# Two blocks of conditioned mixers and expert layers on one core: convolution taps without GpSimd, residual rows scaled in other stages

## The chip, the cores and the metric

The kernel runs on one core of a Trainium2 chip. The metric is the device time of one execution in microseconds. Engines are named TensorE (PE in the rows), VectorE (DVE), ScalarE (ACT), GpSimd (POOL) and SyncE (SP, which only issues DMAs and takes part in no arithmetic).

## The reference

512 tokens of width 1024 pass a first block (a state space and attention mixer, then an expert layer) and a second block of two layers, each with a mixer and an expert layer. The second block has 256 context tokens beside the 512. What the change touches:

```python
def conv_mixers(h, w_in, w_out, a_dw_w, a_dw_b, a_ln_g, a_ln_b, b_dw_w):
    z = h @ w_in
    a_val, a_gate, b_gate, c_gate, b_val = jnp.split(z, CONV_SPLITS, axis=-1)
    ya = a_val * jax.nn.sigmoid(a_gate)
    ya = depthwise_conv(ya, a_dw_w) + a_dw_b          # 31 taps, 512 channels
    ya = jax.nn.silu(layer_norm(ya, a_ln_g, a_ln_b))
    yb = b_gate * depthwise_conv(c_gate * b_val, b_dw_w)   # 3 taps
    return jnp.concatenate([ya, yb], axis=-1) @ w_out
...
# second block, each layer
x_lat = layer_norm(DEEPNORM_ALPHA_2 * x_lat + g1 * y_lat, ln1_g[i], ln1_b[i])
h_lat = x_lat * (1.0 + sc2) + sh2
...
y = hier_moe(h_lat.reshape(-1, d), *moe_w).reshape(x_lat.shape)
x_lat = layer_norm(DEEPNORM_ALPHA_2 * x_lat + g2 * y, ln2_g[i], ln2_b[i])
```

The expert layer picks one group of experts and two experts in it for each token, so each expert of width 512 sees its own few tokens. The first layer norm's result is wanted twice: modulated, by the experts, and as it is, as the residual of the second norm. The residual rows are this result with gain and bias (`ln`) multiplied and added.

## The kernel before

Weights stay f32 in memory; for the projections a weight tile and its input are split into a rounded high part (`wh`, `xh`, ScalarE) and the rest (`wl`, `xl`, VectorE, the subtraction of L245), and three matmuls (`xh` `wh`, `xl` `wh`, `xh` `wl`) replace one. All weights are loaded in pieces of 128 x 2048 f32 (1 MB) by SyncE, in program order, into `raw` (four buffers) and, in the expert layers, `rawx` (eight more).

The span in order: mixer 1 (0 to 350), expert layer m1 (selection 366 to 388, run to 694, combination 698 to 748), `conv_layer` (748 to 1003) and its output projection, m2 (selection 1090 to 1138, run to 1697, combination to 1780), grouped query attention (`G.attend`), the projection for neighbourhood attention (`na_proj`) and that attention (`na`, 2066 to 2157), output projection, m3 (selection 2226 to 2265, run to 2690), final combination.

*Convolution.* `proj(u)` computes unit u of the input projection for four blocks of 128 channels, over 512 latent and 256 context columns (L1445, L1446). Unit 0 is a gate, unit 1 makes `AB`, the padded input of the 31 taps. The first `POOL_TAPS` = 7 taps are done by GpSimd, a product and a sum each (L1500, L1502), into a second accumulator; VectorE does the other 24 (L1505, L1508) and adds the two (L1511). Units 2 to 4 go on beside the taps; a scheduler has set the order of each engine, and VectorE's accumulates alternate with the `wl` subtractions of later units.

*Expert layers.* `Moe.start` opens pools and starts the first loads, `select` computes the routing and the index tables `midx`, `mtok`, `midn`, and `run` goes over S places, S = 32 in m2 and 26 in m3. An expert with few tokens has a place of H rows ("narrow", H = 32 in m2 and m3), the others 128 rows ("wide"); two or three places are double. The weights of the first two places, experts 0 and 1, are loaded before the routing is known, and they are wide in any case. A wide place cuts its weights into `wh` and `wl`, a narrow one multiplies gate and up weights straight from the loaded slot (L1208). GpSimd gathers a place's token rows (L1110, three buffers `xg`) and scatters its results (L1187 wide, L1238 narrow). `run` calls `step` so that gather, loads and matmuls of neighbouring places overlap, and calls `beside` once, at j = 10.

*Residual rows.* In `affine_rows` the function `keep` scales a tile of 128 normed rows on GpSimd with gain and bias (L1406, L1407); for m2 and m3 it is called between `start` and `select`, and for m2 the result goes to `xd2` in DRAM (L1409), where the end of the run picks it up. The residual of the convolution layer is scaled in m1's combination (L1900, L1901) and stored to `x2d`. The residual of the attention layer lies in `x3d`, and is loaded and scaled in `na` (L2021 to L2023).

## Time and profile before

| | us |
|---|---|
| median of 3 runs | 2746.97 (2745.14 to 2748.28) |
| the profiled execution, its own time | 2732.68 |
| its span | 2731.0 |
| TensorE busy | 2296.8 (84%) |
| VectorE busy | 1630.4 (60%) |
| ScalarE busy | 1075.3 (39%) |
| GpSimd busy | 541.5 (20%) |
| DMA, mean over the span | 244 GB/s, 666 MB |
| mean granted clock of TensorE | 0.921 |

Busy time counts from an instruction's start to its end, also where it stands still in between. A stage's limit is therefore read in the stage: which engine is busy all along, or which wait ends last there. In the rows "[6.36 <-DVE pt L663]" says that the engine sat idle for 6.36 us before this instruction and that VectorE's write of `pt` at line 663 ended it. Counts like "x6" group instructions that follow each other without a gap.

### The profile page before, as it was taken

To read this page: it belongs to the slowest core of one execution; us is meant where nothing else is said; L and a number is where in the kernel's file an instruction comes from. 1 tells how busy PE (TensorE), PEld (TensorE's weight loads), DVE (VectorE), ACT (ScalarE), POOL (GpSimd) and SP (SyncE) were. 2 spreads that over 40 slices of the span, in tenths; PEclk is the share of its full clock that TensorE was granted. 3 is DMA by queue.
4 is the path that set the end of the run, shared out by engine and by line. 5 is a ranking of instruction groups with operands and counts; after the bars stand their busy time and mean duration, and the time that the engine had idled before them with its cause. 6 is when DMAs were issued, how large, how long until landed. Compare 5 with 4: busy or idle time off the path is not lost. (4 is left out here: it accounts for less than half of the span.)

```text
span 2731.0 us, 33393 instructions
## 1 busy us (share of the span) xinstructions
PE 2296.8 (84%) x12255; PEld 1565.0 (57%) x12255; DVE 1630.4 (60%) x2357; ACT 1075.3 (39%) x1564; POOL 541.5 (20%) x479
## 2 busy tenths in 40 slices
PE   8999979998597799399988988399997757989991
PEld 6845547555286657276655655255684456766661
DVE  5536467454649967785455445666557687444445
ACT  4432237454411143175455445433322325444442
POOL 0122011100339513411111110110003131111112
PEclk9999989999798899699999999699998878999996
DMA  5222579998421145599999897621234346999993
GB/s 191 96 86 70 199 285 380 389 363 306 173 80 59 35 166 195 223 360 420 363 409 400 325 394 274 231 95 62 97 120 145 129 185 260 391 417 412 421 416 140
DMA packets 115257, 666.43 MB, mean 244 GB/s; under 512 B 21229, under 2 KB 22489, under 8 KB 44944
## 3 DMA queue, kind: packets, MB, share of 16 engines
q1 hardware_dynamic: 86960, 604.02, 56.9%
q10 hardware_dynamic: 11712, 30.81, 3.4%
q0 software_dynamic: 16416, 29.41, 3.0%
q8 instruction: 99, 1.62, 0.2%
q14 instruction: 70, 0.57, 0.1%
HBM read 646.27 MB, written 45.38 MB: 253 GB/s over the span
## 5 line engine op out<-in xcount | busy, mean ns | idle before, releaser
L245 DVE TENSOR_TENSOR wl<-raw,wh 128x1024 fp32r<-128x1024 f32 (+1 forms) x241 | 298.1, 1272 | 269.1 <-ACT wh L244 266.7
L245 DVE TENSOR_TENSOR wl<-rawx,wh 128x1024 fp32r<-128x1024 f32 x312 | 367.3, 1222 | 148.3 <-ACT wh L244 145.6
L272 PE MATMUL ps<-wh,xh 128*128 128x512 f32 (+1 forms) x864 | 335.4, 417 | 66.4 <-ACT wh L244 60.1
L273 PE MATMUL ps<-wl,xh 128*128 128x512 f32 (+1 forms) x864 | 352.0, 407 | 15.3 <-DVE wl L245 14.5
L244 ACT CAST wh<-rawx 128x1024 fp32r<-128x1024 f32 x312 | 311.3, 1049 | 94.6 <-PE ps L274 35.6
L274 PE MATMUL ps<-wh,xl 128*128 128x512 f32 (+1 forms) x864 | 346.2, 402 | 1.1 <-DVE xl L245 1.1
L244 ACT CAST wh<-raw 128x1024 fp32r<-128x1024 f32 (+1 forms) x241 | 244.4, 1051 | 187.5 <-PE ps L274 61.3
L272 PEld LDWEIGHTS ps<-wh,xh 128*128 128x128 f32 x864 | 168.7, 200 | 131.5 <-ACT wh L244 82.6
L273 PEld LDWEIGHTS ps<-wl,xh 128*128 128x128 f32 x864 | 172.1, 199 | 62.7 <-DVE wl L245 29.4
L274 PEld LDWEIGHTS ps<-wh,xl 128*128 128x128 f32 x864 | 171.3, 199 | 35.9 <-DVE xl L245 2.2
L1286 PE MATMUL adaps<-raw,ccs 128*2 128x512 f32 x352 | 165.0, 595 | 1.3 <-ACT adrow L1289 1.3
L1110 POOL DMA_INDIRECT xg<-xr,mtok x79 | 83.3, 1055 | 372.7 <-PE ps L1197 196.1
L273 PE MATMUL ps<-wl,ah 128*128 128x512 f32 x352 | 143.0, 406 | 13.8 <-DVE wl L245 13.8
L272 PE MATMUL ps<-wh,ah 128*128 128x512 f32 x352 | 142.1, 404 | 11.1 <-ACT wh L244 9.3
L274 PE MATMUL ps<-wh,al 128*128 128x512 f32 x352 | 137.7, 394 | 0.2 <-DVEq L1085 0.2
L1508 DVE SCALAR_TENSOR_TENSOR acc<-AB,cols,acc 128x783 f32<-128x783 f32 x92 | 130.7, 1463 | 0.5
L245 DVE TENSOR_TENSOR xl<-ps,xh 128x512 fp32r<-128x512 f32 x88 | 58.2, 687 | 107.6 <-ACT xh L244 107.5
L1185 ACT COPY y<-ps 128x512 f32<-128x512 f32 x88 | 51.7, 588 | 129.8 <-PE ps L274 129.8
L272 PE MATMUL ps<-wh,MH 128*128 128x512 f32 x224 | 90.0, 406 | 13.0 <-ACT wh L244 13.0
L273 PE MATMUL ps<-wl,MH 128*128 128x512 f32 x224 | 90.6, 404 | 3.3 <-DVE wl L245 3.2
L274 PE MATMUL ps<-wh,ML 128*128 128x512 f32 x224 | 90.5, 404 | 0.0
L272 PEld LDWEIGHTS ps<-wh,ah 128*128 128x128 f32 x352 | 66.7, 190 | 40.5 <-ACT wh L244 19.8
(583 smaller groups left out, 4387.1 us busy)
## 6 DMA issues: line engine op xcount, KB each, us to landing
rawx<-in_m_dram SPq DMA_DIRECT2D x296, 1024.0 KB
raw<-in_m_dram SPq DMA_DIRECT2D x148, 1024.0 KB
raw<-in_ada_dram SPq DMA_DIRECT2D x44, 1024.0 KB
raw<-in_w_dram SPq DMA_DIRECT2D x10, 1024.0 KB
raw<-in_cw_dram SPq DMA_DIRECT2D x10, 1024.0 KB
raw<-in_aw_dram SPq DMA_DIRECT2D x8, 1024.0 KB
xr<-rh SPq DMA_DIRECT2D x14, 512.0 KB
yt<-m2y SPq DMA_DIRECT2D x6, 1024.0 KB
```

The costliest lines, as they stand in the source:

```text
L244: self.nc.scalar.copy(hi, src)
L245: self.nc.vector.tensor_sub(lo, src, hi.bitcast(F32))
L272: nc.tensor.matmul(ps, ah, bh, start=start, stop=False)
L273: nc.tensor.matmul(ps, ah, bl, start=False, stop=False)
L274: nc.tensor.matmul(ps, al, bh, start=False, stop=stop)
L1110: nc.gpsimd.indirect_dma_start(out=xg[-1], out_offset=None, in_=self.xrows, in_offset=bass.IndirectOffsetOnAxis(ap=gi[0:n], axis=0), bound ...
L1185: nc.scalar.copy(y[:, h * 512:(h + 1) * 512], p)
L1286: nc.tensor.matmul(p[0:2], K.cc[:, k], raws[k // 4][:, (k % 4) * 512:(k % 4 + 1) * 512], start=k == 0, stop=k == 7)
L1508: nc.vector.scalar_tensor_tensor(acc[:, cb], AB[:, cb, j:j + 783], K.col("adw", j * 4 + cb), acc[:, cb], op0=OP.mult, op1=OP.add)
```

## The change

It has five parts.

1. Convolution: the first `PE_TAPS` = 4 taps are matmuls with a diagonal matrix of the tap's weights on TensorE (`taps`), which ScalarE builds and whose sums it writes to `acc` with the bias; VectorE does the other 27. GpSimd does none. The pool of the cut weight quarters has six buffers instead of four.
2. The residual rows of the convolution layer leave m1's combination unscaled and are loaded, scaled and stored again after unit 0 of the convolution's projection (`between`).
3. The residual rows of m2 go to `xd2` unscaled, behind each tile's norm; from j = 10 of m2's run on, each j loads one tile, scales it on GpSimd and stores it (`leave`, `keep`). m3's tiles are scaled at the same j, where they lie. The buffers `cuts` of m2 become five.
4. x3's rows are loaded, scaled and stored at the end of `G.attend`; `na` only loads them, on SyncE's queue.
5. `few=True` in m2 and m3: the first two places are narrow (an overflow goes to further blocks). In `select` two loops over tiles become single instructions.

```diff
-POOL_TAPS = 7
+PE_TAPS = 4
...
     def run(self, res, pre, beside=lambda j: None):
...
-            if j == 10:
-                beside()
+            beside(j)
...
-        nar = i is not None and self.P <= i < self.S
+        nar = i is not None and (self.P <= i < self.S or self.few and i < 2)
...
-    def keep():
-        nc.gpsimd.tensor_mul(r, r, K.gb[0])
-        nc.gpsimd.tensor_add(r, r, K.gb[1])
+    def keep(pool=None):
+        v, x = r, xd if xd is None else xd[t * 128:(t + 1) * 128]
         if xd is not None:
-            K.stores.append(lambda: nc.sync.dma_start(xd[t * 128:(t + 1) * 128], r))
+            v = pool.tile([128, D], F32, name="kept")
+            nc.sync.dma_start(v, x)
+        nc.gpsimd.tensor_mul(v, v, K.gb[0])
+        nc.gpsimd.tensor_add(v, v, K.gb[1])
+        if xd is not None:
+            nc.sync.dma_start(x, v)
     K.rows.push(lambda: rows(nc.vector))
+    if xd is not None:
+        nc.sync.dma_start(xd[t * 128:(t + 1) * 128], r)
...
-        S_ = Scope(tc, "c0s", bufs=4)
+        S_ = Scope(tc, "c0s", bufs=6)
...
+            def taps(cb):
+
+                dg = W.tile([128, PE_TAPS, 128], F32, name="diag", bufs=2)
+                p, q = K.ps(), K.ps()
+                for j in range(PE_TAPS):
+                    nc.scalar.mul(dg[:, j], K.ident, K.col("adw", j * 4 + cb))
+                    for d, o, n in ((p, j, T), (q, j + 527, TC)):
+                        nc.tensor.matmul(d[:, 0:n], dg[:, j], AB[:, cb, o:o + n], start=j == 0, stop=j == PE_TAPS - 1)
+                nc.scalar.activation(acc[:, cb, 0:T], p, AF.Identity, bias=K.col("adb", cb))
+                nc.scalar.activation(acc[:, cb, 527:783], q[:, 0:TC], AF.Identity, bias=K.col("adb", cb))
...
             proj(0, gate(AF.Sigmoid))
+            between(W)
             proj(1, aval)
+            taps(3)
...
-            for j in range(POOL_TAPS + 1, 31):
+            for j in range(PE_TAPS, 31):
...
-        for cb in range(4):
-            nc.vector.tensor_add(acc[:, cb], acc[:, cb], a2[:, cb])
...
-    m2 = Moe(K, 6, 32, 8, A["m2"], A["rw2"], A["rb2"], xr2, "m2", 32, 18, 32, 2)
-    m3 = Moe(K, 4, 32, 8, A["m3"], A["rw3"], A["rb3"], xr3, "m3", 26, 11, 32, 3, cuts=4)
+    m2 = Moe(K, 6, 32, 8, A["m2"], A["rw2"], A["rb2"], xr2, "m2", 32, 18, 32, 2, cuts=5, few=True)
+    m3 = Moe(K, 4, 32, 8, A["m3"], A["rw3"], A["rb3"], xr3, "m3", 26, 11, 32, 3, cuts=4, few=True)
...
+        def between(W):
+            gb = [K.bcast(W, A["ln"][i:i + 1], D, "gb%d" % i) for i in (2, 3)]
+            for t in range(4):
+                r = W.tile([128, D], F32, name="x2")
+                x = tile_of(x2d)(t)
+                nc.sync.dma_start(r, x)
+                nc.gpsimd.tensor_mul(r, r, gb[0])
+                nc.gpsimd.tensor_add(r, r, gb[1])
+                nc.sync.dma_start(x, r)
...
+    def leave(j, li, pool=None):
+        if j == 10:
+            K.gb = raw_rows([A["ln"][i:i + 1] for i in (li, li + 1)])
+        if j >= 10 and K.left:
+            K.left.pop(0)(pool)
...
                 G.attend(W, Oc)
+                gb3 = ln_rows(W, 6)
+                for t in range(4):
+                    r, x = W.tile([128, D], F32, name="x3", bufs=2), x3d[t * 128:(t + 1) * 128]
+                    nc.sync.dma_start(r, x)
+                    nc.gpsimd.tensor_mul(r, r, gb3[0])
+                    nc.gpsimd.tensor_add(r, r, gb3[1])
+                    nc.sync.dma_start(x, r)
...
-            nc.scalar.dma_start(x3r[64 * i:64 * i + 64, t], x3d.rearrange("(c r) d -> r c d", r=8)[2 * t + i])
-        nc.gpsimd.tensor_mul(x3r[:, t], x3r[:, t], got["gb3"][0])
-        nc.gpsimd.tensor_add(x3r[:, t], x3r[:, t], got["gb3"][1])
+            nc.sync.dma_start(x3r[64 * i:64 * i + 64, t], x3d.rearrange("(c r) d -> r c d", r=8)[2 * t + i])
```

The order on GpSimd ahead of m2's run, before: `lnrs` are steps of the norm, `xt` the rows of the convolution layer's result, `rh` gain and bias, `xg0` to `xg2` the buffers of the gather.

```order
L291 TENSOR_TENSOR lnrs_7564<-lnrs_7564,mhalf_101 128x1
L1406 TENSOR_TENSOR xt_6978<-xt_6978,rh_7677 128x1024 x4
L1407 TENSOR_TENSOR xt_6978<-xt_6978,rh_7679 128x1024 x4
L1406 TENSOR_TENSOR xt_6978<-xt_6978,rh_7677 128x1024 x2
L1407 TENSOR_TENSOR xt_6978<-xt_6978,rh_7679 128x1024 x2
L1110 DMA xg0_7698<-xr2_115,mtok_98 128x1024
```

The same place on GpSimd after the change.

```order
L1041 MEMSET xg1_7703 128x1024
L1041 MEMSET xg2_7704 128x1024
L288 TENSOR_SCALAR lnrs_7571<-lnmv_7569 128x1
L289 TENSOR_TENSOR lnrs_7571<-lnrs_7571,mhalf_99 128x1
L1109 DMA xg0_7702<-xr2_113,mtok_96 32x1024
```

The twelve scaling operations have left the place between the norm and the first gather, and this gather fetches 32 rows.

On GpSimd in m2's run, about the first double place, before: `m2y` is what the layer's results are scattered to, through `midx` by wide places and `midn` by narrow ones.

```order
L1238 DMA m2y_121<-y_9515,midn_100 6144x256
L1110 DMA xg0_7698<-xr2_115,mtok_98 128x1024
L1187 DMA m2y_121<-y_9647,midx_97 1536x1024
L1110 DMA xg1_7699<-xr2_115,mtok_98 32x1024
L1187 DMA m2y_121<-y_9657,midx_97 1536x1024
L1238 DMA m2y_121<-y_9865,midn_100 6144x256
```

After the change, the same place; `kept` is a reloaded tile, `rawx_9434` the slot with gain and bias.

```order
L1237 DMA m2y_119<-y_9323,midn_98 6144x256
L1109 DMA xg0_7702<-xr2_113,mtok_96 128x1024
L1409 TENSOR_TENSOR kept_9437<-kept_9437,rawx_9434 128x1024
L1410 TENSOR_TENSOR kept_9437<-kept_9437,rawx_9434 128x1024
L1186 DMA m2y_119<-y_9463,midx_95 1536x1024
L1109 DMA xg1_7703<-xr2_113,mtok_96 32x1024
L1186 DMA m2y_119<-y_9473,midx_95 1536x1024
L1409 TENSOR_TENSOR kept_9610<-kept_9610,rawx_9434 128x1024
L1410 TENSOR_TENSOR kept_9610<-kept_9610,rawx_9434 128x1024
```

Pairs of scaling operations stand between gathers and scatters, six in all; the second one stands behind the second scatter of the double place.

On SyncE at the same stage of m2's run, after the change; before, only the weight loads (`in_m2_dram`) stand there.

```order
L1876 DMA rawx_9434<-in_ln_dram 128x1024 x2
L1408 DMA kept_9437<-xd2_117 128x1024
L232 ISA
L232 DMA rawx_9482<-in_m2_dram 128x2048
L232 ISA
L232 DMA raw_9484<-in_m2_dram 128x2048
L1412 DMA xd2_117<-kept_9437 128x1024
```

Two weight loads stand between the reload of a tile and its store; the next loads come behind the store.

## Rows read from the trace of the kernel before

**Rows 1.** table by stretch: length, busy us (instructions) by engine, clock, DMA share, GB/s
```profile
748.00:793.00 45.00, 44.75 (x246) 38.99 (x247) 10.89 (x11) 11.90 (x17) 0.52 (x9) 0.96 0.39 140
793.00:928.00 135.00, 98.37 (x528) 84.63 (x526) 134.64 (x98) 18.38 (x23) 130.69 (x52) 0.88 0.10 32
1190.00:1320.00 130.00, 120.80 (x819) 83.27 (x818) 72.11 (x72) 68.98 (x94) 18.36 (x18) 0.97 1.00 415
1320.00:1350.00 30.00, 27.92 (x176) 21.00 (x178) 14.18 (x17) 14.51 (x21) 2.97 (x3) 1.00 0.80 318
1577.60:1612.00 34.40, 28.98 (x194) 18.85 (x190) 17.08 (x17) 16.38 (x22) 3.99 (x5) 0.95 1.00 393
1866.00:1920.00 54.00, 54.00 (x221) 29.49 (x221) 28.84 (x51) 22.11 (x36) 2.83 (x4) 1.00 0.12 40
```

**Rows 2.** timeline (start, us, instructions), selection of mixture 2, VectorE then GpSimd
```profile
1090.51 0.18 DVE L789 TENSOR_REDUCE g_m<-L 128x6 f32<-128x24 f32 x1
...
1097.39 13.76 DVE L874 TENSOR_TENSOR le<-L,g_eq 128x32 f32<-128x32 f32 x6
...
1138.34 0.15 DVE L1022 TENSOR_SCALAR midn<-midx 32x14 int32<-32x14 int32 x1
...
1088.03 9.29 POOL L1406 TENSOR_TENSOR xt<-xt,rh 128x1024 f32<-128x1024 f32 x4 [8.43 <-DMA rh<-in_ln_dram]
...
1111.07 4.63 POOL L1407 TENSOR_TENSOR xt<-xt,rh 128x1024 f32<-128x1024 f32 x2
```

**Rows 3.** timeline, selection of mixture 1, VectorE
```profile
366.48 0.17 DVE L789 TENSOR_REDUCE g_m<-L 128x4 f32<-128x16 f32 x1
...
387.55 0.15 DVE L1022 TENSOR_SCALAR midn<-midx 64x6 int32<-64x6 int32 x1
```

**Rows 4.** groups of VectorE, 793 to 928: count, busy us, mean ns, idle before
```profile
L1508 DVE SCALAR_TENSOR_TENSOR acc<-AB,cols,acc 128x783 f32<-128x783 f32 x67 | 105.7, 1625 | 0.2
```

**Rows 5.** timeline, VectorE, after GpSimd's taps
```profile
941.71 6.69 DVE L1508 SCALAR_TENSOR_TENSOR acc<-AB,cols,acc 128x783 f32<-128x783 f32 x7
```

**Rows 6.** timeline, TensorE, end of the convolution
```profile
967.58 3.60 PE L1286 MATMUL adaps<-raw,ccs 128*2 128x512 f32 x8
...
973.50 2.93 PE L339 MATMUL ps<-acc,ones 128*128 128x512 f32 x4 [2.32 <-DVE acc L1511]
```

**Rows 7.** groups of VectorE, combination of mixture 1, 698 to 748
```profile
L292 DVE SCALAR_TENSOR_TENSOR lnrs<-lnmv,lnrs 128x1 f32<-128x1 f32 x4 | 4.9, 1230 | 2.7 <-POOL lnrs L291 2.6
```

**Rows 8.** timeline, SyncE's queue, then TensorE, start of mixture 2's run
```profile
1103.53 37.63 SPq L1409 DMA_DIRECT2D xd<-xt  x6
...
1146.40 26.66 SPq L234 DMA_DIRECT2D rawx<-in_m_dram  x8
...
1175.00 14.21 SPq L234 DMA_DIRECT2D raw<-in_m_dram  x4
...
1149.29 0.76 PE L272 MATMUL ps<-wh,xh 128*128 128x512 f32 x1 [4.99 <-ACT xh L244]
```

**Rows 9.** timeline, GpSimd, second half of the first double place
```profile
1357.84 1.02 POOL L1187 DMA_INDIRECT m2y<-y,midx  x1 [6.42 <-DMA m2y<-y,midx]
```

**Rows 10.** timeline, selection of mixture 3, VectorE
```profile
2226.43 0.17 DVE L789 TENSOR_REDUCE g_m<-L 128x4 f32<-128x16 f32 x1
...
2264.65 0.16 DVE L1022 TENSOR_SCALAR midn<-midx 32x15 int32<-32x15 int32 x1
```

**Rows 11.** timeline, neighbourhood attention, VectorE then TensorE
```profile
2075.47 11.62 DVE L663 TENSOR_TENSOR pt<-pt,pt 128x256 f32<-128x256 f32 x7
...
2123.06 2.96 DVE L663 TENSOR_TENSOR pt<-pt,pt 128x256 f32<-128x256 f32 x7
...
2086.81 2.30 PE L679 MATMUL po<-pt,ones 128*64 128x512 f32 x4 [6.36 <-DVE pt L663]
...
2109.31 2.21 PE L679 MATMUL po<-pt,ones 128*64 128x512 f32 x4 [7.33 <-DVE pt L663]
```

More of the change, by code (lines that the diff above doesn't have):

```diff
@@ L1045, in start, with run @@
         K.extra = None
-    def run(self, res, pre, beside=lambda: None):
+    def run(self, res, pre, beside=lambda j: None):
         K, nc, tc, S, nd = self.K, self.K.nc, self.K.tc, self.S, self.dbl
@@ L1937, in build @@
     m2.start(B)
-    K.stores = []
-    for f in K.left:
-        f()
     with tc.tile_pool(name="adrp", bufs=1) as K.adrp:
@@ L1945, in build @@
         m2.select(rt.p)
-    for f in K.stores:
-        f()
     rt.close()
@@ L1955, in pre2, with beside2 @@
         nc.sync.dma_start(got[0], ada[0].row(5, 0).to_broadcast([128, D]))
+    def beside2(j):
+        if j == 10:
+            ada[0].finish(5, 6)
+        leave(j, 4, kb.p)
     with tc.tile_pool(name="adrp", bufs=1) as K.adrp:
-        m2.run(xd2, pre2, lambda: ada[0].finish(5, 6))
+        m2.run(xd2, pre2, beside2)
     B.close()
+    kb.close()
     os = Scope(tc, "aoc")
@@ L2050, in build @@
                      lambda t, lag: affine_rows(K, rt.p, m3, xt[:, t], sb[0], K.rcols[0], t, lag), m3.lag)
-    K.gb = [K.bcast(rt.p, A["ln"][i:i + 1], D, "rh", bufs=3) for i in (8, 9)]
     B = ExitStack()
     m3.start(B)
-    K.stores = []
-    for f in K.left:
-        f()
     m3.select(rt.p)
@@ L2064, in pre3 @@
         got["g2"] = raw_rows([ada[1].row(5, 0)])[0]
-    m3.run(None, pre3)
+    m3.run(None, pre3, lambda j: leave(j, 8))
     B.close()
```

54 lines of the change are left out of this document (18 added, 36 removed).

## The prediction

> **What bounds the kernel now.** The page's slices first: no engine bounds the whole span, so the stages were read one by one, in the table by stretch [rows 1]. In the convolution VectorE is busy 134.64 of 135 us and GpSimd 130.69, TensorE only 98.37. In a mixture layer's run the DMA share is 1.00 at 415 GB/s, and a pair of a wide and a narrow place takes 34.4 us with TensorE at 28.98 and VectorE at 17.08. Grouped query attention (1866 to 1920) is TensorE alone, 54.00 of 54. Then each stage where GpSimd works was read on VectorE's own line in order of time, because its instructions change their length there.
>
> What the reader is to see: a VectorE operation with two inputs in SBUF stands still while a GpSimd `tensor_tensor` runs. In the selection of mixture 2 GpSimd scales residual rows from 1088.03 to 1115.7, and VectorE's six products of 128x32 take 13.76 us, 2.29 each, the length of the GpSimd operation (9.29 for four) [rows 2]. In mixture 1, with GpSimd idle, the whole selection from the first maximum to the last index goes from 366.48 to 387.70, 21.2 us [rows 3]; in mixture 2 from 1090.51 to 1138.5, 48.0 us [rows 2]. In the convolution an accumulate takes 1625 ns on the mean beside GpSimd [rows 4] and 6.69/7 = 0.956 us without it [rows 5].
>
> **The change part by part.** All terms are made against the profiled execution (span 2731.0, time 2732.68 us).
>
> *Convolution taps.* GpSimd loses 28 products and 24 sums, all of its 130.69 us, and VectorE four first taps and four final sums; VectorE then does 108 accumulates instead of 92. The 67 that stand beside GpSimd save 67 x (1.625 - 0.956) = 45 us [rows 4, 5], the eight lost operations about 1 us each, the 16 added cost 15: 37 less, so VectorE could end its accumulates at 973.5 - 37 = 936. The end is where TensorE's sums over the channels start [rows 6]. TensorE gets 16 taps by a diagonal matrix, each 512 and 256 columns of f32. The f32 matmuls of an `ada` unit take 3.60 us for eight records, two to a matmul of 512 columns [rows 6]: 0.90, and half of that for 256, so 16 x 1.35 = 22 us. The projections' pairs of 512 and 256 columns take 44.75/123 = 0.364 us [rows 1]; 96 pairs a unit and five units are 175 us. From 748, where the first one starts, that is 748 + 175 + 22 = 945 if TensorE never waits, later than VectorE's 936, and 28 below 973.5. TensorE idles 37 us of 135 now [rows 1]; a part may stay, since weight differences still stand between accumulates in VectorE's order, although six quarter buffers instead of four let half a unit more be cut ahead. I take 5 us of waits, as VectorE has the room: **-23**, bounds -28 and -8 (20 us of the waits stay).
>
> *Combination of mixture 1.* Its eight residual operations leave. VectorE's four one-column normalisation steps take 1230 ns there [rows 7], where 0.17 is usual for so small an operation [rows 3]: 4.2 us, and GpSimd's own steps of the normalisation no longer stand behind a 2.3 us operation. **-6**, bounds -3 and -12. The reload, scaling and store now stand under the projections; the store holds SyncE ahead of weight loads of units that come 35 us and more later: nothing, unless a tile's round trip takes over 10 us.
>
> *Selection of mixture 2 and first places.* GpSimd's 12 operations leave. After them 22.7 us of selection are left (1115.8 to 1138.5), and what stands before takes under 2 us at 0.17 to 0.2 an operation: 48.0 becomes 24.4, **-24**, merged products included. The weight stream stands still too: SyncE's six stores of the scaled rows last until 1141, and it restarts at 1146.40 [rows 8]. The next 12 loads (12.6 MB) go until 1189, 42 us where 415 GB/s makes 30, because the first wide place has its first matmul only at 1149.29 and holds the slots; a narrow place multiplies its gate and up weights straight out of the loaded slot, without their cuts. **-12**, bounds 0 and -12. Together -36.
>
> *Residual rows inside the run of mixture 2.* This is the cost. From the tenth place on six reloads, GpSimd pairs and stores stand between weight loads, and one slot holds the two norm rows. Bytes: 1 + 6 x 1.05 = 7.3 MB, at 415 GB/s 17.6 us, in a stage whose DMA share is 1.00 [rows 1]. SyncE holds each store until its GpSimd pair (4.6 us, [rows 2]) is done, and behind it stand the weight loads of the next places; the pair stands in GpSimd's order between gathers and scatters, the second one behind the scatter of the double place's second half, at 1357.84 now [rows 9]. Two loads are issued between a reload and its store, and earlier ones are still in flight. Bounds: 10 us, if the double place, where the share falls to 0.80 [rows 1], takes part of the bytes, and 18 + 6 x 4.6 + 13 = 59, if every pair stops the stream and the double place adds a wait of 13. I take 30, nearer the lower end, since the eleven slots left hold 11 x 2.5 = 28 us of loads against a stop of 4.6. Net of mixture 2: -36 + 30 = **-6**, from -26 to +23.
>
> *Mixture 3.* 38.4 us of selection [rows 10] come down to mixture 1's 21.2: **-17**, from -23 to -8. The eight GpSimd operations in its run touch tiles that stay in SBUF, with no store on SyncE; two rows of 0.5 MB are 2.5 us of DMA, and the narrow first places are taken to give these back.
>
> *Neighbourhood attention.* Beside x3's scaling seven products take 11.62 us, later 2.96, and TensorE's row sums wait 6.36 and 7.33 us for them [rows 11]: -14. The reload, eight operations and stores stand beside grouped attention now, where TensorE has no idle time but VectorE has 25 of 54 us [rows 1]; there too a stretch of 8.7 us per four operations may reach TensorE. I take +4, bounds 0 and +14: **-10**. VectorE's stops agree with a rule of the Trainium skill ("SBUF — State Buffer", section "Who interferes with whom"): a VectorE instruction with two SBUF inputs and a GpSimd instruction that reads SBUF shut each other out for the whole instruction, and the order of issue decides who loses. That rule speaks against the change where work is only moved: if each stop reached the end in attention and the convolution, it would give the first rival's sum instead of mine.
>
> Merged products in mixture 1: -0.5. Together: -23 - 6 - 6 - 17 - 10 - 0.5 = **-62.5 us**, 2670 for the profiled execution. The median of the runs, 2746.97, lies 14.3 above it; the same distance is kept: 2746.97 - 62.5 = 2684.5.
>
> **The rivals.**
>
> 1. *The stops move along with GpSimd's work.* For: 36 operations of 2.3 us, 84 us, are moved and not removed, and VectorE stops beside them wherever they stood so far. Against: in a mixture's run VectorE has 17 us idle of 34.4 [rows 1], room for two pairs of 4.6. Grouped attention has no idle TensorE, and the first projections cut their weights on VectorE: the full 14 instead of 4 in attention, and 10 in the convolution (half of eight operations): 2684.5 + 20 = 2704.5.
> 2. *TensorE becomes the convolution's bound with its waits kept.* If the taps' 22 us come on top of the present waits, the stage ends where it did: 2684.5 + 23 = 2707.5. For: the differences still follow accumulates. Against: these take 37 us less.
> 3. *The reloads in mixture 2 are hidden.* The cost is 10 instead of 30: 2664.5. For: the slots' reserve. Against: a share of 1.00.
> 4. *The reloads stop the stream until TensorE has drained it* (slower). If GpSimd's pair waits behind a gather that waits for TensorE, loads and places follow each other: six places pay their 17.2 us twice, 103, plus the bytes, 18. That is 121 instead of 30: 2684.5 + 91 = 2775.5. It decides from 92 us in all, some 12 for each of the six beside the bytes. For: the pair's position in GpSimd's order. Against: a gather runs places ahead of TensorE.
>
> That the first two places outgrow their narrow form is no rival: the reference's router gives those experts fewer than 32 tokens.
>
> **How the numbers follow.** Forecast 0.48; rivals 1 to 4: 0.15, 0.10, 0.20, 0.05; 0.02 for several adverse ends at once that leave no change. The unknown terms, added as independent (mixture 2 some 25, convolution 15, the others 6 to 8), reach 33 us to either side; the first three rivals lie inside, and 2775.5 is left out: **2648 to 2718**. A measurement of this kernel tells about 0.2% (5.5 us) from no change. Faster by more: 0.92; within: 0.02; slower: 0.06.
>
> **What would show it.** In the convolution accumulates of 0.96 us throughout and sums over channels that start near 950 on the old scale. Selection of mixture 2 in 24 us and of mixture 3 in 21. SyncE's first load in mixture 2 near 1122, and a run no more than 20 us longer from there than now. Row sums in neighbourhood attention that wait under 1 us. The prediction is wrong if accumulates stay at 1.4 us without GpSimd, if TensorE stops in grouped attention for over 10 us, or if SyncE waits 10 us or more at each store in mixture 2.

## The result, and the profile after

The changed kernel takes **2678.89 us** (median of four runs, 2667.56 to 2688.86) against 2747.62 (2745.14 to 2753.45) for the kernel before in the same comparison: a ratio of **0.9748, interval [0.9727, 0.9769]**, 68.7 us less. Forecast were 62.5 us less and 2684.5. The profiled execution of the changed kernel took 2677.64 us, its span is 2675.6.

The page of the changed kernel, span and busy time by engine:

```profile
span 2675.6 us, 33526 instructions
...
PE 2290.1 (86%) x12407; PEld 1538.8 (58%) x12407; DVE 1489.5 (56%) x2273; ACT 1029.7 (38%) x1532; POOL 418.2 (16%) x428
```

GpSimd lost 123 us of busy time and VectorE 141, TensorE 7. As before, this says little; the stages tell. The table by stretch of the changed kernel, with the columns of [rows 1]: the convolution, the first part of mixture 2's run, the stretch in which residual rows are reloaded (four windows), grouped attention.

```profile
784.00:919.00 135.00, 135.00 (x713) 111.46 (x712) 120.80 (x134) 24.05 (x38) 4.79 (x2) 1.00 0.15 51
1088.00:1230.00 142.00, 122.11 (x887) 78.66 (x880) 68.38 (x69) 66.87 (x91) 17.83 (x18) 0.93 1.00 410
1230.00:1260.00 30.00, 26.32 (x158) 19.13 (x156) 12.66 (x14) 12.21 (x17) 3.99 (x4) 0.89 0.50 201
1260.00:1290.00 30.00, 27.05 (x175) 19.32 (x173) 10.14 (x15) 11.23 (x18) 7.77 (x5) 1.00 0.71 272
1290.00:1320.00 30.00, 20.58 (x125) 13.43 (x124) 10.52 (x11) 8.86 (x12) 10.29 (x6) 0.83 0.66 258
1320.00:1350.00 30.00, 21.78 (x130) 14.24 (x130) 12.67 (x12) 11.61 (x16) 12.50 (x8) 0.89 0.81 307
1848.00:1902.00 54.00, 53.52 (x213) 28.30 (x213) 37.89 (x50) 21.63 (x36) 21.56 (x10) 1.00 0.35 132
```

The convolution has changed hands: TensorE is busy 135.00 of 135 where it was 98.37 [rows 1], VectorE 120.80 where it was full. In mixture 2 the stream of weights, without a break until 1230 (share 1.00), falls to 0.50, 0.71, 0.66 and 0.81 as soon as the reloads begin, and TensorE follows with 20.58 of 30 us.

To set stage against stage, both kernels were profiled once more on one chip, one after the other (runs r_before and r_after). Each length below goes from one landmark of the trace to the next: VectorE's first product on `yt` in m1's combination, first matmul of the convolution's projection, last accumulate, first maximum of m2's selection, its last index, last scatter of the run, first matmul of grouped attention's scores, end of the third of its four groups of row sums, first matmul of the output projection behind neighbourhood attention, then m3's selection and run in the same way. The last row joins two stretches without a change, that output projection (64.9) and what follows m3's last scatter (48.0).

| stage, us | before | after | difference | forecast | first pair of profiles |
|---|---|---|---|---|---|
| all up to m1's combination | 698.7 | 705.0 | +6.3 | -0.5 | +0.5 |
| combination of m1 | 42.5 | 32.7 | -9.8 | -6 | -9.8 |
| convolution | 224.5 | 200.8 | -23.7 | -23 | -23.3 |
| output projection, norm | 115.7 | 116.5 | +0.8 | 0 | -2.5 |
| selection of m2 | 46.1 | 27.5 | -18.6 | -24 | -20.4 |
| to m2's first matmul, and its run | 576.4 | 593.1 | +16.8 | +18 | +36.3 |
| combination of m2, projections | 103.7 | 103.1 | -0.6 | 0 | -0.4 |
| grouped attention | 115.1 | 115.1 | 0 | +4 | +1.4 |
| projections, neighbourhood attention | 230.2 | 213.3 | -16.9 | -14 | -17.5 |
| selection of m3 | 37.0 | 21.1 | -15.9 | -17, with the run | -17.2 |
| to m3's first matmul, and its run | 418.5 | 411.2 | -7.3 | | -3.0 |
| output projection, and the rest | 112.9 | 112.8 | -0.1 | 0 | +0.5 |
| span | 2721.3 | 2652.2 | **-69.1** | **-62.5** | -55.4 |

The first row holds no changed instruction but the merged products of m1's selection. In the executions seen m1's selection began at 362 to 367 us and its run took 292 to 296, whichever kernel it was, and the 6.3 us come from these two. The first pair of profiles comes from the runs behind the page above and the page of before; its 55.4 is less than the 68.7 of the medians because the profiled execution of before lay 15 us under its median and that of the changed kernel 1 us under its own. The last column shows which terms hold from one execution to the next: all but the run of m2 agree within 6 us, and it differs by 20.

### The profile page after: what moved, and what is told of

Same layout as the page of the kernel before. It is cut to its first block, busy times and chain, and to the rows that moved or that the text cites. A ratio compares the mean times of both kernels' runs of the same rounds, so it can differ in the third digit from the quotient of the medians.

```text
span 2675.6 us, 33526 instructions
## 1 busy us (share of the span) xinstructions
PE 2290.1 (86%) x12407; PEld 1538.8 (58%) x12407; DVE 1489.5 (56%) x2273; ACT 1029.7 (38%) x1532; POOL 418.2 (16%) x428
## 5 line engine op out<-in xcount | busy, mean ns | idle before, releaser
L243 DVE TENSOR_TENSOR wl<-raw,wh 128x1024 fp32r<-128x1024 f32 (+1 forms) x225 | 282.3, 1294 | 259.7 <-ACT wh L242 258.9
L243 DVE TENSOR_TENSOR wl<-rawx,wh 128x1024 fp32r<-128x1024 f32 x280 | 341.0, 1266 | 153.5 <-ACT wh L242 152.0
L270 PE MATMUL ps<-wh,xh 128*128 128x512 f32 (+1 forms) x800 | 312.3, 425 | 103.5 <-ACT wh L242 103.5
L271 PE MATMUL ps<-wl,xh 128*128 128x512 f32 (+1 forms) x800 | 337.2, 421 | 19.0 <-DVE wl L243 18.1
L272 PE MATMUL ps<-wh,xl 128*128 128x512 f32 (+1 forms) x800 | 329.5, 413 | 0.3 <-DVE xl L243 0.3
L242 ACT CAST wh<-rawx 128x1024 fp32r<-128x1024 f32 x280 | 278.3, 1048 | 43.8 <-DMA rawx<-in_m_dram 23.8
L242 ACT CAST wh<-raw 128x1024 fp32r<-128x1024 f32 (+1 forms) x225 | 227.2, 1051 | 162.7 <-PE ps L272 50.2
L1207 PE MATMUL ps<-rawx,xh 128*32 128x256 f32 (+1 forms) x1440 | 115.5, 411 | 1.0 <-ACT xh L1198 1.0
L1520 DVE SCALAR_TENSOR_TENSOR acc<-AB,cols,acc 128x783 f32<-128x783 f32 x108 | 106.4, 1031 | 5.9 <-issue 5.0
L1234 PE MATMUL ps<-rawx,ah 128*32 128x256 f32 (+1 forms) x864 | 95.5, 411 | 0.0
```

The lines of the kernel that those rows point to most:

```text
L242: self.nc.scalar.copy(hi, src)
L243: self.nc.vector.tensor_sub(lo, src, hi.bitcast(F32))
L270: nc.tensor.matmul(ps, ah, bh, start=start, stop=False)
L271: nc.tensor.matmul(ps, ah, bl, start=False, stop=False)
L272: nc.tensor.matmul(ps, al, bh, start=False, stop=stop)
L1207: nc.tensor.matmul(p[j * n:(j + 1) * n], x[:, c * n:(c + 1) * n], r[:, o:o + w], start=c == 0, stop=c == 7)
```

## The experiments

### Do GpSimd's instructions stretch VectorE's, or their writes, or does the work itself take so long?

The forecast rests on one reading: a VectorE instruction with two inputs in SBUF stands still while GpSimd runs a `tensor_tensor`. Two kernels give GpSimd work beside the convolution of the changed kernel that nobody wants, behind unit 1 of the projection. The one reads and adds, the other only writes.

```diff
+        junk = W.tile([128, D], F32, name="x2")[:, 0:783]
+        for j in range(48):
+            nc.gpsimd.tensor_add(junk, AB[:, j % 4, 0:783], AB[:, j % 4, 1:784])
```

> The changed kernel with 48 sums of 128x783 added on GpSimd beside VectorE's accumulates; they read the padded input of the taps and write to a tile that nothing uses, so the result is the same. Theory A (a GpSimd operation that reads SBUF stops VectorE's two-input operations): the accumulates beside it take 1.5 to 1.6 us instead of about 1.0, and the end of the accumulates comes 25 to 35 us later than in the changed kernel (939.7 there). Rival (accumulates were slow because of TensorE's or ScalarE's traffic, or by the mixing with weight differences): they stay at 1.0 and the end moves by less than 5 us.

```diff
+        junk = W.tile([128, D], F32, name="x2")
+        for j in range(96):
+            nc.gpsimd.memset(junk, 0.0)
```

> As the run with 48 added sums, but with 96 memsets of 128x1024 on GpSimd, 0.95 us each by the traces, so about as long in all; they only write SBUF. Theory A as the Trainium skill has it (SBUF — State Buffer, Who interferes with whom: only a GpSimd instruction that reads SBUF contends with a two-input VectorE instruction): accumulates stay at about 1.0 us and the stage's end within 3 us of the changed kernel's. Rival (any GpSimd access stops VectorE): they stretch as beside the sums, 25 to 35 us more.

Groups of VectorE and of GpSimd in the stage (730 to 992), kernel with added reads (count, busy us, mean ns, idle before):

```profile
L1523 DVE SCALAR_TENSOR_TENSOR acc<-AB,cols,acc 128x783 f32<-128x783 f32 x108 | 158.3, 1509 | 5.9 <-issue 5.0
...
L1520 POOL TENSOR_TENSOR x<-AB 128x783 f32<-128x783 f32 x48 | 100.7, 2099 | 30.8 <-DVE AB L1478 24.5 <-DMA x2d<-x 2.8
```

The same view of the kernel with added writes:

```profile
L1523 DVE SCALAR_TENSOR_TENSOR acc<-AB,cols,acc 128x783 f32<-128x783 f32 x108 | 106.3, 1031 | 5.9 <-POOL x L1520 5.0
...
L1520 POOL MEMSET x<- 128x1024 f32 x96 | 91.6, 955 | 8.2 <-DMA x2d<-x 2.7
```

About as much GpSimd time (100.7 and 91.6 us) makes the accumulates half as long again in the one case (1509 ns, [rows 4] had 1625) and leaves them at 1031 in the other. The stage went from 200.8 to 255.4 us with reads, 55 more where 25 to 35 were expected (108 accumulates, each 0.48 us longer, make 52), and was 200.0 with writes; the single runs took 2706.19 and 2649.81 us beside 2654.21 for the changed kernel (on another chip). Of these two kinds of GpSimd work the one that reads SBUF stops VectorE, and the one that only writes does not. That is the rule of the Trainium skill that the prediction named ("SBUF — State Buffer", section "Who interferes with whom"): a VectorE instruction with two SBUF inputs contends with a GpSimd instruction that reads SBUF and not with one that only writes. Here the trace agrees, 1509 ns against 1031.

### What shortened the convolution: GpSimd's leaving, or the taps on TensorE?

This kernel does the four taps on VectorE, all 31 there, none on TensorE.

```diff
-                if cb:
-                    taps(cb - 1)
...
-            taps(3)
...
-            for j in range(PE_TAPS, 31):
+            nc.vector.tensor_scalar(acc[:, cb], AB[:, cb, 0:783], K.col("adw", cb), K.col("adb", cb),
+                                    op0=OP.mult, op1=OP.add)
+            for j in range(1, 31):
```

> The changed kernel without the taps on TensorE: VectorE does all 31, none on GpSimd. Theory A (taking GpSimd out is what shortens the stage; TensorE's taps only save VectorE 16 operations of 1 us): the accumulates end 6 to 16 us later than in the changed kernel (939.7 after a start of the projections at 739.0, so 200.7 long), and at most 217 long, still well under the 224 of the kernel before. Rival (the gain comes from the taps on TensorE): as long as before, 224 or more. If TensorE bounds the stage, the end moves by less than 5 us, as its 22 us are gone too.

It took 2648.25 us (one run). The stage, from the first projection to the last accumulate, is 202.3 us, 1.5 longer than with the taps on TensorE. TensorE's timeline at its end shows who binds now:

```profile
903.90 2.74 PE L337 MATMUL ps<-acc,ones 128*128 128x512 f32 x8
906.57 7.03 PE L1285 MATMUL adaps<-raw,ccs 128*2 128x512 f32 x16
921.93 2.93 PE L337 MATMUL ps<-acc,ones 128*128 128x512 f32 x4 [8.33 <-DVE acc L1517]
```

The projections are done at 903.9, 171.6 us after their start at 732.3 and not 193.1 as in the changed kernel; TensorE then fills up with other weights and waits for VectorE's accumulates. So the 16 taps cost TensorE 21.5 us, the forecast's 22, and nearly all of the stage's gain is GpSimd's leaving: 22.2 of 23.7 us are there without TensorE's help. The stage ends within 2 us either way, bound by TensorE in the changed kernel and by VectorE here: the last of the outcomes named ahead.

### Why is the run of m2 longer?

The forecast gave the reloads 30 us. Two theories could explain the lengthening seen (42 us from first matmul to last scatter in the first pair): the store of a scaled tile holds SyncE's queue and with it the weights; or the reloads themselves (bytes, GpSimd's place in its own order, VectorE stopped) cost it. SyncE's timeline of the changed kernel, the first reload, and the third:

```profile
1229.43 0.43 SPq L1408 DMA_DIRECT2D kept<-xd  x1
1230.60 0.34 SPq L232 DMA_DIRECT2D rawx<-in_m_dram  x1
1236.94 0.34 SPq L232 DMA_DIRECT2D raw<-in_m_dram  x1
1269.12 0.33 SPq L1412 DMA_DIRECT2D xd<-kept  x1
...
1300.95 3.23 SPq L232 DMA_DIRECT2D rawx<-in_m_dram  x4
1304.22 0.50 SPq L1408 DMA_DIRECT2D kept<-xd  x1
1304.96 0.45 SPq L232 DMA_DIRECT2D rawx<-in_m_dram  x1
1305.62 0.35 SPq L232 DMA_DIRECT2D raw<-in_m_dram  x1
1323.21 0.33 SPq L1412 DMA_DIRECT2D xd<-kept  x1
```

GpSimd's timeline beside it:

```profile
1263.19 1.01 POOL L1109 DMA_INDIRECT xg<-xr,mtok  x1 [4.79 <-PE ps L1196]
1264.23 2.40 POOL L1409 TENSOR_TENSOR kept<-kept,rawx 128x1024 f32<-128x1024 f32 x1
1266.71 2.38 POOL L1410 TENSOR_TENSOR kept<-kept,rawx 128x1024 f32<-128x1024 f32 x1
...
1293.65 1.86 POOL L1186 DMA_INDIRECT m2y<-y,midx  x1 [4.66 <-ACT ah L1226]
1295.52 2.40 POOL L1409 TENSOR_TENSOR kept<-kept,rawx 128x1024 f32<-128x1024 f32 x1
...
1318.41 2.35 POOL L1409 TENSOR_TENSOR kept<-kept,rawx 128x1024 f32<-128x1024 f32 x1 [15.53 <-DMA kept<-xd]
1320.84 2.34 POOL L1410 TENSOR_TENSOR kept<-kept,rawx 128x1024 f32<-128x1024 f32 x1
```

SyncE issues nothing from 1237.3 to 1269.1 and from 1306.0 to 1323.2. The first two holds are GpSimd's order: the first pair stands behind a gather that TensorE releases at 1263.19 (rival 4's mechanism), the second one behind the scatter of the double place's second half, at 1293.65 (the order that the prediction read from [rows 9]). The other four are the reload's own way. The third one is issued at 1304.22 behind four weight loads of 1 MB (from 1300.95 on), which take 10 us at 415 GB/s, lands 14 us later (at 1318.41, where its pair starts), and only then can the pair run. The six holds are 31.8, 22.9, 17.2, 17.4, 15.3 and 17.5 us, 122 in all; the forecast had set 4.6 us for one. What TensorE gets of it stands in its own timeline, with ScalarE, which cuts the loaded weights, as the releaser:

```profile
1308.21 1.22 PE L270 MATMUL ps<-wh,xh 128*128 128x512 f32 x2 [8.68 <-ACT wh L242]
```

Four kernels test the theories. One issues each store one place later, behind the next place's loads:

```diff
         if xd is not None:
-            nc.sync.dma_start(x, v)
+            return lambda: nc.sync.dma_start(x, v)
...
+        if j == 10:
+            K.late = None
+        late, K.late = K.late if j >= 10 else None, None
         if j >= 10 and K.left:
-            K.left.pop(0)(pool)
+            K.late = K.left.pop(0)(pool)
+        if late is not None:
+            late()
```

> The changed kernel, but in the run of mixture 2 each scaled tile is stored one place later, behind the next tile's reload; the bytes, the GpSimd pairs and the slot held for gain and bias stay. Theory A (SyncE stands at each store until its GpSimd pair is done, and the weight stream stands behind it): SyncE's six holds, 122 us together in the changed kernel (32, 23, 17, 17, 16 and 17), fall under 15 in all, and the run of mixture 2, 605.8 us there, falls to about 570; time about 2643. Theory B (the 7.3 MB and the lost slot are the price, the holds are covered by loads in flight): the run stays within 8 us of 605.8, time 2671 to 2687. Theory C (GpSimd's pairs stop the weight differences on VectorE): also unchanged, with VectorE's differences as long as before.

One leaves the reload, scaling and store of m2's rows out:

```diff
-        if j == 10:
+        if j == 10 and li == 8:
...
-        if j >= 10 and K.left:
+        if j >= 10 and K.left and li == 8:
```

> The changed kernel without the reload, scaling and store of mixture 2's residual rows and without the load of their gain and bias: this part of the computation is left out, the residual stays unscaled. It gives the whole price of that part. Theory A: the run of mixture 2 falls from 605.8 to about 552, that is 36 us of holds and 18 of bytes below, time about 2625. Theory B: it falls by the bytes and the slot alone, some 20 us, to 586, time about 2659.

One issues the stores late and scales on VectorE in the runs of m2 and m3 (the lines of the first one, and):

```diff
-        nc.gpsimd.tensor_mul(v, v, K.gb[0])
-        nc.gpsimd.tensor_add(v, v, K.gb[1])
+        nc.vector.tensor_mul(v, v, K.gb[0])
+        nc.vector.tensor_add(v, v, K.gb[1])
```

> The changed kernel with the stores of mixture 2 one place later, and with the residual rows of mixtures 2 and 3 scaled in the runs by VectorE instead of GpSimd. Theory A (in some executions one weight difference on VectorE stands through GpSimd's eight operations of mixture 3, 17.8 us, and in others the two engines take turns; that makes the run of mixture 3 424 or 410 us and scatters the times by 25): no VectorE operation over 6 us in the run of mixture 3, its run 409 to 412 us, the run of mixture 2 no longer than 583, four times within 12 us of each other, about 2650. Theory B (mixture 3's run varies for another reason, in the DMA): 424 us again or times as far apart as before.

And one scales on VectorE, likewise in both runs, and gives the store to ScalarE's queue, so that SyncE waits at none (`nc.scalar.dma_start(x, v)`, at once):

> Scaling of the residual rows of mixtures 2 and 3 in the runs by VectorE, and mixture 2's stores issued by ScalarE right behind their pair, so that SyncE has no store in its order; reloads stay on SyncE. Theory A (the holds on SyncE that are left with a store one place later, 13 to 18 us each, still stop the stream): the run of mixture 2 is 5 to 15 us shorter than the 570.4 of that run, and the ratio to the kernel before falls under 0.965, to about 0.960. Rival (with one place of delay the loads in flight cover what is left): within 4 us of 570.4 and a ratio of 0.963 to 0.967.

Measured, with the run counted from the end of m2's selection to its last scatter, so that all versions are counted alike:

| kernel | ratio to before, interval | holds of SyncE at stores | selection to last scatter | TensorE's idle time, first matmul to last scatter |
|---|---|---|---|---|
| before (two profiles) | 1 | none | 574.1, 576.4 | 60 |
| changed (two profiles) | 0.9748 [0.9727, 0.9769] | 122, 113 | 610.4, 593.1 | 102, 92 |
| store late | 0.9670 [0.9641, 0.9699] | 54 | 588.1 | 87 |
| no reload | 0.9642 [0.9626, 0.9658] | none | 581.2 | 80 |
| late, on VectorE | 0.9649 [0.9630, 0.9668] | 89 | 574.9 | 77 |
| on VectorE, store on ScalarE | 0.9686 [0.9672, 0.9700] | none | 576.0 | 80 |

Idle time is the length of the run less TensorE's busy time in it, from rows such as this one of the kernel with late stores on VectorE:

```profile
1085.80:1656.20 570.40, 493.27 (x3202) 332.70 (x3202) 292.17 (x295) 268.41 (x364) 67.59 (x65) 0.95 0.93 374
```

Against what was expected: with the stores late the holds fell to 54 us and not under 15, and the run from its first matmul to 583.3 and not to 570; without the reloads it took 576.6, where one theory had 552 and the other 586; late on VectorE it took 570.4, under the 583 set for it; with the store on ScalarE 571.3, within the rival's 4 us, at a ratio a little above the rival's.

One caution comes first. Three more kernels, those of the sections on the convolution, hold the changed kernel's code for this stage, and took 588.8, 596.4 and 590.8 us in it. So five executions of the same code lie between 588.8 and 610.4, with holds of 109 to 122 us, while each of the other versions was profiled once.

Three things follow. The reloads cost the changed kernel 14 to 36 us of the run (588.8 to 610.4 against 575), and a version with the reloads still there has it all back: bytes are not the price. Moving the stores alone helps by the times (0.9670 against 0.9748, intervals apart), while its 588.1 us lie at the short end of what the unmoved stores gave; moving the scaling to VectorE as well took another 13 us off the stage in one profile each, but the two ratios, 0.9670 and 0.9649, can't be told apart. The length of the holds alone doesn't set the price: with late stores and the scaling on VectorE SyncE is still held for 89 us, until VectorE comes to the pair in its own order, but six weight loads (15 us) go out ahead of each hold but the first, of 13 to 17 us, and no idle time of TensorE over 3 us is left in that run (28 us in such stretches in the changed kernel, 20 in its second profile, 7 with the stores late).

The last kernel, without holds at stores and no faster, bears this out but doesn't prove it. SyncE stands there too, between 1215 and 1400 for 61 us until VectorE has cut the weights in a slot, up to 15.6 at a time. And the store now holds ScalarE, which cuts weights: three times a cut waits for VectorE's pair, 7.6 us in all, and TensorE's two stretches over 3 us (4.29 each) stand at two of these. ScalarE's timeline of this kernel:

```profile
1306.48 1.99 ACT L242 CAST wh<-rawx 128x1024 fp32r<-128x1024 f32 x2 [3.57 <-DVE kept L1410]
```

Which part of GpSimd's share is the pair's place among gathers and which its stopping VectorE isn't settled: VectorE's weight differences in the run lost only 5 us in all (1258 against 1221 ns in 128).

One more kernel undoes the move: m2's rows are scaled in the selection and stored there, as before, and nothing in the run.

```diff
+    def old():
+        nc.gpsimd.tensor_mul(r, r, K.gb[0])
+        nc.gpsimd.tensor_add(r, r, K.gb[1])
+        K.stores.append(lambda: nc.sync.dma_start(xd[t * 128:(t + 1) * 128], r))
...
-        K.left.append(keep)
+        K.left.append(keep if xd is None else old)
...
+    K.gb = [K.bcast(rt.p, A["ln"][i:i + 1], D, "rh", bufs=3) for i in (4, 5)]
...
+    for f in K.left:
+        f()
...
+    for f in K.stores:
+        f()
```

> The changed kernel with mixture 2's residual rows scaled where the kernel before did it, between start and selection, stored after the selection; all else as changed. Theory A: the selection goes back from 27.5 to about 48 us, the first matmul of the run comes another 4 us later, and the run falls to about 552: 2679 + 25 - 54 = 2650, so this part of the change alone costs about 29 us. Rival (the first two narrow places bring nothing without the early start, and the run goes back to the 563 of the kernel before): 2679 + 25 - 43 = 2661. If the selection stays near 27 us, GpSimd's operations were not what stretched it.

It took 2669.52 us (2661.68 to 2677.12), ratio 0.9725 [0.9702, 0.9748], where the changed kernel has 0.9748. The selection is 40.6 us again (about 48 expected) and the first matmul 2.6 us later; the run from there took 570.3, neither the 552 nor the 563 expected, and selection to last scatter is 577.5. From the first maximum to the last scatter: 618.1 here, 620.6 and 638.0 in the changed kernel, 622.1 and 622.5 before; the other three executions of the changed stage gave 615 to 624. **The move of m2's rows alone brings nothing**: its 13 us in the selection and 2.6 behind it are given back in the run. With the stores late and the scaling on VectorE the same stretch is 602.8, and there the move pays 15, in one profile of each.

A sixth kernel scales m2's rows where they lie, on VectorE, in the output projection ahead of the router:

```diff
+    def kept():
+        nc.vector.tensor_mul(r, r, K.gb[0])
+        nc.vector.tensor_add(r, r, K.gb[1])
...
+    if xd is not None:
+        K.rows.push(kept)
```

Its `cuts` buffers in m2 are six, as the reload's tiles are gone.

> The changed kernel with mixture 2's residual rows scaled by VectorE in the output projection of the convolution, right behind each tile's norm, and stored once, so nothing of it is left in the run; six cut buffers in mixture 2 as in the kernel before; mixture 3's rows scaled in its run by VectorE. Theory A (five cut buffers instead of six are why the run without any reload still took 576.6 us): the run of mixture 2 falls to 562 to 567. Rival (the buffers don't matter, the stream and TensorE hold each other up after the double places): 574 to 578. The output projection may take 0 to 6 us more, VectorE having 25 us idle of 80 there. Time about 2635 by theory A, 2647 by the rival.

It took 2674.76 us (2670.39 to 2676.42), ratio 0.9794 [0.9774, 0.9813]. The scaling comes ahead of the router's second step and changes the rows that this step and the experts see, so its result differs, its experts hold other tokens, and its run of m2 (591.9 us) can't be set against the others. Whether five `cuts` buffers instead of six lengthen that run, the question of this kernel, therefore stays open. What can be read is the stage with the scaling: the output projection took 107.4 us instead of 93.9, VectorE's new work lay on the path there, 13.5 us and as dear as the selection was.

### The narrow first places

```diff
-    m2 = Moe(K, 6, 32, 8, A["m2"], A["rw2"], A["rb2"], xr2, "m2", 32, 18, 32, 2, cuts=5, few=True)
-    m3 = Moe(K, 4, 32, 8, A["m3"], A["rw3"], A["rb3"], xr3, "m3", 26, 11, 32, 3, cuts=4, few=True)
+    m2 = Moe(K, 6, 32, 8, A["m2"], A["rw2"], A["rb2"], xr2, "m2", 32, 18, 32, 2, cuts=5)
+    m3 = Moe(K, 4, 32, 8, A["m3"], A["rw3"], A["rb3"], xr3, "m3", 26, 11, 32, 3, cuts=4)
```

> The changed kernel with the first two places of mixtures 2 and 3 wide again, as before. Theory A (a wide first place holds the loaded slots and delays the restart of the stream): in mixture 2 the first matmul comes 6 us later after the selection, and the first twelve loads end some 12 us later; in mixture 3 3 and 4 us: time about 2704 at most. Rival (the runs are bound by DMA and take the same bytes either way, so only the first matmul moves): 9 us, 2688.

2696.57 us (2693.99 to 2698.79), ratio 0.9817 [0.9801, 0.9833]: by the times this kernel is 0.7 per cent, some 19 us, slower than the changed one. The traces give a smaller sum for the places: first matmul 2.0 us later in m2 and 2.3 in m3, m2 from selection to last scatter 610.6 against 588.8 to 610.4, m3's run 428.3 against 410.6 and 406.7. The time lay between the two that were expected. In m2 they gain nothing beyond what an execution varies. Of m3's 18 us most is the stop of one VectorE instruction that the last section describes, which this execution had and the changed kernel's had not; what is left is within the scatter. The four times of this kernel lie within 5 us, so that the stop may have come in all four, and then most of the 19 us are its price. What the places are worth isn't shown.

The traces do show what becomes of an early start of m2. TensorE begins 4.6 us behind the selection with narrow first places, 6.6 with wide ones and 10.8 before. But the first 100 us of the run, without the reloads, with wide places, and before, read (columns as in [rows 1]):

```profile
1079.08:1179.08 100.00, 88.28 (x684) 56.49 (x684) 47.08 (x48) 47.35 (x66) 14.27 (x14) 0.94 1.00 407
1083.27:1183.27 100.00, 99.95 (x597) 74.65 (x598) 76.56 (x75) 71.17 (x89) 15.05 (x14) 0.98 0.93 372
1149.29:1249.29 100.00, 98.91 (x585) 73.50 (x586) 71.55 (x71) 67.03 (x84) 13.28 (x12) 0.96 0.90 360
```

With narrow places the DMA share is 1.00 and TensorE stands for 12 of the 100 us, waiting for cuts of weights just loaded; with wide ones it stands for 0 to 1 at a share of 0.90 to 0.93. The early start is waited away, at least in part, within 100 us.

### The two profiles on one chip

> The kernel before once more, for a profile on the same chip as the next one. Theory A (the run of mixture 2 has one length for one program): 563 us from first matmul to last scatter. Rival (the run's length goes with the execution, since the two engines' stops and the stream's gaps fall differently): more than 8 us away from 563.

> The changed kernel once more on the same chip. In the first profile the run of mixture 2 took 605.8 us; with the same code for that stage it took 584 and 592 in the runs with added GpSimd work in the convolution. Theory A (the price of the reloads is the holds on SyncE, whatever the execution): 584 to 606 us, and against the kernel before on this chip 20 to 43 more. For mixture 3: 407 to 411 us if VectorE and GpSimd take turns, 424 if one weight difference stands through all eight operations.

2722.99 and 2654.21 us; the kernel before had a median of 2724.17 on this chip. From first matmul to last scatter the run of m2 took 565.5 us before (2 from the 563) and 588.5 after, 23 more, at the low end of what was expected; m3's took 406.7. The stages stand in the table at the top.

## Why the prediction was right

**Convolution** (forecast -23, -23.7 measured). The mechanism held: accumulates of 1031 ns throughout (forecast 956; the seven of [rows 5] were a little fast), TensorE as the new bound, taps of 21.5 us (22). The exact agreement has luck in it. Where 5 us of waits were set, TensorE didn't wait at all from its first projection to its last, and without the taps the projections took 171.6 us instead of 175; against these 8 us stand as many that the sum left out, VectorE's last operations and its last accumulate, which come behind the last projection (932.0 to 939.7 in the first profile). Rival 2, the waits kept, is refuted by 135.00 of 135.

**Combination of m1** (-6, -9.8): the mechanism was right, the term too small. The normalisation steps of [rows 7] went from 1230 to 160 ns, and GpSimd's steps of the norm stand behind nothing now.

**Selection of m2** (-24, -18.6 and -20.4): mechanism right; 3 us went to a new wait. The forecast priced VectorE's line alone. VectorE has everything ready at 1061.5, and then waits for matmuls that stand on TensorE behind a unit of `ada`. VectorE's timeline, then TensorE's, of the changed kernel:

```profile
1055.38 0.18 DVE L787 TENSOR_REDUCE g_m<-L 128x6 f32<-128x24 f32 x1
...
1065.54 0.36 DVE L976 COPY cc<-ps 128x192 f32<-128x192 f32 x1 [4.02 <-PE ps L901]
...
1082.76 0.16 DVE L1022 TENSOR_SCALAR midn<-midx 32x32 int32<-32x32 int32 x1
```

```profile
1057.85 7.03 PE L1285 MATMUL adaps<-raw,ccs 128*2 128x512 f32 x16 [0.66 <-ACT adrow L1288]
1064.81 0.19 PE L901 MATMUL ps<-Ab,sub 128*128 128x32 bf16 x1
```

L901 begins 9.4 us after the first maximum. In the kernel with all taps on VectorE TensorE took `ada` matmuls earlier, while it waited for the accumulates; there L901 began 6.2 us after the maximum and the selection took 24.2 us, the forecast's 24.4.

**The run of m2** (forecast -12 for an early stream and +30 for the reloads; +16.8 and +36.3 measured). The sum, +18, lies near the one and below the other, but the first step failed: no version was clearly shorter than before from the end of its selection, not even those without holds (574.9 to 581.2 against 574.1 and 576.4). The stream does run at a share of 1.00 from the first matmul on, but that brought no earlier end: the forecast let TensorE use the earlier loads at once, and it stood for 12 of the first 100 us instead. What gives back the rest of the time was not tried by itself. And the price of the reloads was built on a wrong size: holds of 15 to 32 us where 4.6 were set, of which the loads in flight and the slots hid most. The forecast took a hold to be as long as GpSimd's pair. It left out that the reload itself queues behind the weight loads issued ahead of it and gave a wait at the double place only to its upper bound. In the second pair of profiles the two steps are off by +12 and -13 us, so that the sum is right by luck; in the first by +12 and +6. The condition that the prediction named against itself, SyncE waiting 10 us or more at each store, came true, and rival 4's chain with it for the first store, without rival 4's price.

**m3** (-17; -23.2 and -20.2): the selection came down to 21.1 as m1's had shown, -15.9 and -17.2. The few us more are the first matmul, 2.3 us earlier, and a run that varies by itself.

**Attention** (-10; -16.9 and -16.1). The seven products went from 11.62 to under 3.3 us and TensorE's row sums wait for them once, 0.8 us. VectorE's timeline of the changed kernel, eight products now in one group, then TensorE's:

```profile
2088.17 3.30 DVE L661 TENSOR_TENSOR pt<-pt,pt 128x256 f32<-128x256 f32 x8
```

```profile
2093.55 1.03 PE L677 MATMUL po<-pt,ones 128*64 128x512 f32 x4
```

The +4 for grouped attention didn't come: VectorE is busy 37.89 us of 54 there instead of 28.84 and TensorE still 53.52. Rival 1, stops that move along, is refuted here and in the convolution's first unit; it does hold in m3's run (below).

## What to carry to other kernels

Where VectorE's instructions with two SBUF inputs show a multiple of their usual length, look for GpSimd instructions that read, and take them away from there or do them on VectorE: the kernel with this done in the runs of m2 and m3 as well, and the stores one place late, had the best ratio of those that do all the work, 0.9649 (2634.61 us where before had 2730.46), though not apart from the 0.9670 of late stores alone. A load, compute and store put into a stream of weights costs by its store: in an in-order queue it holds all later loads until its own load, which queues behind what was issued before it, has landed and the engine that computes has come to it in its own order (15 to 32 us here), so issue the store several loads later. When a stage's engine is relieved, price what the next engine in line has standing ahead of the work, as the `ada` unit ahead of the selection's matmuls.

## What the runs showed of the hardware

**One VectorE instruction can lose to GpSimd many times in a row, in some executions and not in others.** In m3's run GpSimd scales four tiles in eight instructions without a gap, and VectorE cuts weights beside it. In the first profile of the changed kernel they alternate; VectorE's and GpSimd's timeline:

```profile
2373.38 12.48 DVE L243 TENSOR_TENSOR wl<-rawx,wh 128x1024 fp32r<-128x1024 f32 x4 [0.21 <-ACT wh L242]
...
2372.42 5.69 POOL L1409 TENSOR_TENSOR xa<-xa,rawx 128x1024 f32<-128x1024 f32 x2 [0.61 <-DMA rawx<-in_ln_dram]
2378.06 6.72 POOL L1410 TENSOR_TENSOR xa<-xa,rawx 128x1024 f32<-128x1024 f32 x2
```

In the kernel with late stores, whose m3 has the same code, one weight difference stood for 17.83 us; VectorE, GpSimd, TensorE:

```profile
2358.76 17.83 DVE L243 TENSOR_TENSOR wl<-rawx,wh 128x1024 fp32r<-128x1024 f32 x1 [0.21 <-ACT wh L242]
...
2357.07 4.68 POOL L1409 TENSOR_TENSOR xa<-xa,rawx 128x1024 f32<-128x1024 f32 x2
2361.70 4.64 POOL L1410 TENSOR_TENSOR xa<-xa,rawx 128x1024 f32<-128x1024 f32 x2
2366.29 4.63 POOL L1409 TENSOR_TENSOR xa<-xa,rawx 128x1024 f32<-128x1024 f32 x2
2370.89 4.62 POOL L1410 TENSOR_TENSOR xa<-xa,rawx 128x1024 f32<-128x1024 f32 x2
...
2376.65 0.79 PE L271 MATMUL ps<-wl,xh 128*128 128x512 f32 x1 [15.38 <-DVE wl L243]
```

GpSimd goes at its full speed (2.3 us each), VectorE's instruction, begun 1.7 us behind the first one, ends 1.1 us behind the eighth, and TensorE stands for 15.38 us. This was seen in the profiles of three kernels (17.8, 17.5 and 17.3 us), and m3's run was 424 to 428 us in them and 405 to 411 in the others. The Trainium skill ("SBUF — State Buffer", section "Who interferes with whom") says that the order of issue decides who loses; here VectorE's instruction, begun within GpSimd's first operation, lost to the seven behind it as well. In the three profiles it began 1.7 to 2.2 us after GpSimd's first operation did. In the six others with these operations a weight difference had begun just before that operation (five) or 0.96 us after its start (one), and the two engines alternated. Whether this offset decides was not tried; which way an execution goes isn't known from its program. Whether this is why the times of the changed kernel lie 21 us apart, those of the kernel with late stores 26, and 6 us where VectorE does the scaling, stays open: the kernels without reloads and with wide first places scale on GpSimd in m3 too, and their times lie 8 and 5 us apart.

**The same program's run of m2 varied** from 588.5 to 605.8 us, first matmul to last scatter, between two executions, with holds of 113 and 122 us, and from 584 to 592 in three kernels with the same code there: a stage that lives on an interplay of queues has no single length, and one profile of it isn't its price.
